# Recurrence outputs turned by VectorE in 32x32 blocks and put together by transfers, with the norm weight applied at the split

## The chip, the cores and the metric

The kernel runs on one core of one Trainium2 chip. The metric is the device time of one execution in microseconds (us), as the median of several runs. The engines are named as in the profile: PE is TensorE (matrix multiply; PEld is its weight load), DVE is VectorE, ACT is ScalarE, POOL is GpSimd, SP is SyncE, which computes nothing here and issues transfers. ACT and POOL issue transfers too; each issuing engine has a queue of its own and works through it in order.

## The reference, cut to what matters

One layer of a hybrid trunk on x of 2048 positions by 1024 channels, all in float32: a pooling branch and a gated recurrence branch, merged by gates, an output projection, a convolutional gated feed-forward layer, and a last norm. The change is in the recurrence branch, between the recurrence's outputs and the projection `w_pb`:

```python
def hgrn2_mixer(zq, zf, zi, zo, lb, norm_g):
    # q, f, k, v of 4 heads of 128 channels; S_t = diag(f_t) S_{t-1} + k_t v_t^T; o_t = S_t^T q_t
    ...
    o = o * lax.rsqrt(jnp.mean(o * o, axis=-1, keepdims=True) + EPS) * norm_g.astype(jnp.float32)
    o = o * jax.nn.silu(heads(zo))
    return o.reshape(B, S, HGRN_WIDTH).astype(zq.dtype)

yb = hgrn2_mixer(zq, zf, zi, zo, lower_bounds[l], hgrn_norm_g[l]) @ w_pb[l]
```

`norm_g` has one weight per channel of a head, the same for all four heads.

## The kernel before, in words

The 2048 positions are worked through in blocks of `TB` = 512. A pass of the outer loop takes two blocks (`b0` and `b0 + 1`, called `hf` 0 and 1): `mixer(b0)` does both branches up to the residual, `ffn(b0)` the feed-forward layer. There are two passes, so two mixers. Products of float32 numbers are split into a high part in the type `fp32r` and a low rest, and done as three matmuls (high-high, high-low, low-high); pairs of blocks are multiplied in a seven-product scheme (`P1` to `P7`), whose sums go through a few PSUM banks (X, Z, V) that VectorE and ScalarE read between the products.

Matmuls of this kind are issued by `mm`, which counts them: after every `MM_PER_TICK` = 6 it runs one `tick`, which converts one more weight tile (`stream.advance`) and steps the waiting tasks. A task is a Python generator; `yield n` lets n ticks pass before it goes on. Weights come through `raw` tiles, loaded on SP's queue (L198) and split by ScalarE (L245) and VectorE (L246) into `ops`. The instructions of each engine are then put in order by a scheduler that follows the program's order and its own estimate of when operands are ready; `first`, `second`, `behind` and `in_turn` are hints of the program to it. The 77 slots of on-chip memory and the eight PSUM banks are handed out the same way.

`hgrn_task(b, h, ...)` does the recurrence for one block and one head; three `runner` tasks work through the eight of a mixer, in between the matmuls of the gate projections (`gr`), so there are 16 in all. The last lines of each task:

- `po` (PSUM) holds the outputs of four chunks of 128 positions side by side: partition = position in the chunk, column = chunk * 128 + channel.
- four DVE instructions (L1169) multiply by the reciprocal root and by the output gate `zt` and write `ot`;
- after four ticks TensorE transposes the four 128x128 squares into the bank `pt` (L1175), so that partition = channel, column = position;
- ScalarE reads `pt` and multiplies by the norm weight, which is a number per partition now (`oh`, L1177), and issues the store to the DRAM tile `od` (`spill`, L987).

`o_task` starts with the second half of the pooling branch's projection (`pa`). It loads the eight `od` on SP's queue into `oT` (`fetch`, L992), waits until `place` reaches `O_PLACE`, and splits them into `oTs` high and low (L680 ScalarE, L681 VectorE), one every two ticks. `branch("pb", ...)` multiplies them by `w_pb`, first two chains of 12 matmuls on the block `hf` 0, then two on `hf` 1, then the rest. While `pa` runs, VectorE's `pa_u` (L1230) reads the bank `pa_Z` between two products that write it.

Of the kernel before, what the change touches and what calls it, by code (L numbers as in the profile page):

```python
# [11 lines left out]
F32 = mybir.dt.float32  # L12
F32R = mybir.dt.float32r
U8 = mybir.dt.uint8
AF = mybir.ActivationFunctionType
ALU = mybir.AluOpType
AX = mybir.AxisListType

P = 128
# [10 lines left out]
TB = 512  # L30
NT = TB // P
# [51 lines left out]
def tile_trunk(  # L83
# [16 lines left out]
    pe, act, dve, pool, sp = nc.tensor, nc.scalar, nc.vector, nc.gpsimd, nc.sync  # L100
# [6 lines left out]
    dram = ctx.enter_context(tc.tile_pool(name="dram", bufs=1, space=bass.MemoryType.DRAM))  # L107
    banks = ctx.enter_context(tc.tile_pool(name="banks", bufs=8, space=bass.MemoryType.PSUM))

    def slot(name, cols=TB, dt=F32):  # L110
        return slots.tile([P, cols], dt, tag="s", name=name, padded_shape=[P, 528])

    def bank(name, cols=512):
        return banks.tile([P, cols], F32, tag="b", name=name, padded_shape=[P, 512])

    def f32(ap):
        return ap.bitcast(F32)
# [467 lines left out]
    ident = const.tile([P, P], F32, tag="ident", name="ident")  # L585
# [9 lines left out]
    o_n1, o_n2, o_bg, o_ps, o_lb, o_hg, o_cb, o_cw = offs  # L595
# [8 lines left out]
    def col(o):  # L604
        return cols[:, o : o + 1]
# [68 lines left out]
    def split(src, name, on_pool=False):  # L674
        hi = slot(name + "h", TB, F32R)
        lo = slot(name + "l", TB, F32R)
        if on_pool:
            up = pool.tensor_scalar(hi, src, 1.0, 0.0, ALU.mult, ALU.add)
        else:
            up = act.copy(hi, src)  # L680
        low = dve.tensor_tensor(lo, src, f32(hi), ALU.subtract)  # L681
        last_split[0] = up, low
        return hi, lo
# [301 lines left out]
    def spill(t, name):  # L985
        d = dram.tile([P, TB], F32, tag=name, name=name)
        act.dma_start(d, t)  # L987
        return d

    def fetch(d, name, eng=sp):  # L990
        t = slot(name)
        eng.dma_start(t, d)  # L992
        return t


    def hgrn_task(b, h, d, q, vd, zd, od):
        def head_of(src, key):
            t = slot(f"{key}{b}_{h}")
            sp.dma_start(t.rearrange("p (c v) -> p c v", c=NT), src[:, :, h * P : (h + 1) * P])
            return t  # L1000
# [166 lines left out]
        ot = slot(f"ot{b}_{h}")  # L1167
        for c in range(NT):
            dve.scalar_tensor_tensor(ot[:, c * P : (c + 1) * P], po[:, c * P : (c + 1) * P],  # L1169
                                     r[:, c : c + 1], zt[:, c * P : (c + 1) * P],  # L1170
                                     ALU.mult, ALU.mult)
        yield 4
        pt = bank(f"pt{b}_{h}")
        for c in range(NT):
            pe.transpose(pt[:, c * P : (c + 1) * P], ot[:, c * P : (c + 1) * P], ident)  # L1175
        t = slot(f"oh{b}_{h}")
        act.activation(t, pt, AF.Copy, scale=col(o_hg))  # L1177
        od[b, h] = spill(t, f"od{b}_{h}")


    go_up, go_io = [False], [False]
# [114 lines left out]
    def add_forms(two, forms, k, name, store=lambda p, t: None, sums=True, pin=lambda i: None,  # L1296
                  eng=pool):

        def comb(p, x0, x1, op):
            if (p, k) in forms or x0 is None or x1 is None:  # L1300
                return
            t = slot(f"{name}_{p}_{k}")
            pin(eng.tensor_tensor(t, x0, x1, op))  # L1303
            forms[p, k] = t
            store(p, t)

        for p, at in (("P1", (1, 0)), ("P2", (1, 1)), ("P4", (0, 1))):
            if (p, k) not in forms and at in two:
                forms[p, k] = two[at]
                store(p, two[at])  # L1310
        if not sums:
            return
        comb("P7", two.get((1, 0)), two.get((0, 0)), ALU.subtract)
        comb("P5", two.get((0, 0)), two.get((0, 1)), ALU.subtract)
        comb("P6", forms.get(("P5", k)), two.get((1, 0)), ALU.subtract)
        comb("P3", forms.get(("P6", k)), two.get((1, 1)), ALU.add)
# [84 lines left out]
    def mixer(b0, forms, late):  # L1401
# [4 lines left out]
        md, od, gd = {}, {}, {}  # L1406
# [11 lines left out]
        def runner():  # L1418
            while taken[0] < 2 * HEADS:
                if queue:  # L1420
                    taken[0] += 1
                    yield from hgrn_task(*queue.pop(0))
                else:
                    yield 1
# [124 lines left out]
        oT = {}  # L1549
# [70 lines left out]
        def evac_b(m, hf, g, ps):  # L1620
            gated(g, hf, g, ps)
            dve.tensor_tensor(y[m, hf], y[m, hf], g, ALU.add)
            if m >= KD // 2 and hf:
                k = m - KD // 2
                two = {(h, r): y[k + r * (KD // 2), h] for h in range(2) for r in range(2)}
                add_forms(two, yf, k, f"yf{b0}", eng=dve)

        def o_task():
            t = {}
            for hf in range(2):  # L1630
                for g in range(HEADS):
                    while (b0 + hf, g) not in od:
                        yield 1
                    t[hf, g] = fetch(od[b0 + hf, g], f"oT{b0 + hf}_{g}")
            while place[0] < O_PLACE:
                yield 1
            for hf in range(2):
                for g in range(HEADS):
                    oT[hf, g] = split(t[hf, g], f"oTs{b0 + hf}_{g}")
                    yield 2  # L1640

        otask = []
        for d in range(2):
            units = [Unit(f"pa{b0}_{2 * d + e}", "pa", emit_a(2 * d + e)) for e in range(2)]
            for p in ORDER:
                place[0] += 1
                if (d, p) == (1, "P1"):
                    otask.append(Task(o_task()))
                for s_, hf in {"P6": ((1, 1),), "P5": ((0, 0),), "P7": ((1, 0),),
                               "P2": ((0, 1),)}.get(p, ()):  # L1650
                    for e in range(2):
                        gate(0, 2 * d + e + KD // 2 * s_, hf)
                while len(pf[FORM[p]]) < 2:
                    place[0] += 1
                    mtask.step()
                w = stream.get("pa")
                for e in range(2):
                    units[e].products(p, pf, pf[FORM[p]], w[:, :, e * 256 : e * 256 + 256])
                    units[e].after(p)
                stream.used(1)  # L1660
# [282 lines left out]
    for b in range(0, SEQ // TB, 2):  # L1943
        forms, task, late = nxt
        if b:
            join(task)
        forms, task, late = mixer(b, forms, late)
        join(task)
        nxt = ffn(b, forms, late)
# [50 lines left out]
```

## Time and profile before

| | |
|---|---|
| median of 3 runs | 2505.35 us (2504.9 to 2505.46) |
| profiled execution, first to last instruction | 2503.3 us |
| median less that span | 2.05 us |
| mean granted TensorE clock in it | 0.999 |
| the first `pt` transposes of the first mixer, the last ones | 199.3 us, 456.8 us |
| the last `pt` transposes of the second mixer | 1694.9 us |
| `pb` of the first mixer starts | 481.3 us |

The profiled execution's own time is known by its span alone. In a row of a group stand line, engine, operation, tiles (out<-in), count, then durations in ns as least / median / most, or busy us and mean ns of one. A row of the timeline begins with its start and its length in us. A row of a wait gives total us, times and the longest. Tile names leave out the numbers of block and head.

### The profile page before, as it was taken

The numbers are of one execution on the slowest core, as the hardware profiler recorded it, in microseconds if no ns is written. First come the engines' busy times: TensorE is split into PE (matmuls) and PEld (weight loads), VectorE is DVE, ScalarE is ACT, GpSimd is POOL, SyncE is SP. The second block draws the span as 40 slices with busy tenths as digits, with TensorE's granted clock in tenths as the row PEclk, the third lists the DMA queues.
The fourth block names the chain that finished last, engine by engine and source line by source line (L and its number), as shares of the span: only waits on it lengthen the run. The fifth ranks groups of instructions, "written<-read, shape, count | busy, mean of one in ns | idle before, by whom it ended". The sixth has DMA issues, their size and how long they took to land.

```text
span 2503.3 us, 35640 instructions
## 1 busy us (share of the span) xinstructions
PE 2490.4 (99%) x11428; PEld 2039.1 (81%) x11428; DVE 1977.8 (79%) x3510; ACT 1201.1 (48%) x2264; POOL 805.1 (32%) x1139
## 2 busy tenths in 40 slices
PE   9999999999999999999999999999999999999998
PEld 7888888888888888888888888887888888888887
DVE  7778768997998778885596777679979887778755
ACT  6534443435555545553554344443365555445534
POOL 4343353403354333451320202223033433325410
PEclk9999999999999999999999999999999999999999
DMA  8888788688888789897344343447443454447852
GB/s 276 271 206 247 227 229 242 210 243 251 202 255 238 226 228 243 263 366 244 122 152 152 118 127 110 143 141 259 135 148 122 153 150 138 149 137 247 319 165 100
DMA packets 257691, 497.68 MB, mean 199 GB/s; under 512 B 26912, under 2 KB 47520, under 8 KB 257184
## 3 DMA queue, kind: packets, MB, share of 16 engines
q1 hardware_dynamic: 189872, 317.53, 40.0%
q0 software_dynamic: 42656, 112.74, 17.7%
q10 hardware_dynamic: 24976, 65.13, 7.5%
q8 instruction: 90, 1.47, 0.2%
q14 instruction: 97, 0.79, 0.1%
HBM read 383.63 MB, written 189.27 MB: 229 GB/s over the span
## 4 chain that ended last, share of the span: by engine, by line
PE 97%; DVE 1%; ACT 0%; DMA 0%; issue 0%; POOL 0%; SPq 0%; ACTq 0%; DVEq 0%
PE dn_P L149 17%; PE up_Z L149 15%; PE up_X L149 10%; PE up_V L149 10%; PE wo_P L149 6%; PE gr_Z L149 5%; PE gr_X L149 4%; PE gr_V L149 4%; PE pb L149 4%; PE io_Z L149 3%; PE fr_Z L149 3%; PE fr_X L149 2%; PE fr_V L149 2%; PE io_V L149 2%; PE pl L1057 2%; PE ur_Z L149 1%
## 5 line engine op out<-in xcount | busy, mean ns | idle before, releaser
L245 ACT CAST ops<-raw 128x512 fp32r<-128x512 f32 x792 | 489.3, 621 | 826.4 <-PE dn_P L149 176.6
L246 DVE TENSOR_TENSOR ops<-raw,ops 128x512 fp32r<-128x512 f32 x792 | 590.4, 749 | 202.8 <-ACT ops L245 198.4
L1734 DVE SCALAR_TENSOR_TENSOR e<-h,cols,e 128x512 f32<-128x512 f32 x176 | 143.4, 819 | 30.9 <-ACT e L1732 23.7
L1732 ACT ACTIVATE e<-h,cols 128x512 f32<-128x512 f32 x176 | 142.2, 814 | 25.1 <-DVE h L1190 18.2
L1737 DVE SCALAR_TENSOR_TENSOR e<-h,cols,e 128x512 f32<-128x512 f32 x176 | 134.0, 771 | 2.5
L992 POOL DMA_DIRECT2D g_P<-dg_P x154 | 83.8, 545 | 160.7 <-PE dn_P L149 112.1
L1303 POOL TENSOR_TENSOR gf_P<-e,e 128x512 f32<-128x512 f32 x44 | 61.1, 1391 | 149.4 <-DVE e L1743 95.9
L467 POOL TENSOR_TENSOR raw<-raw,raw 128x512 f32<-128x512 f32 x36 | 49.1, 1363 | 157.6 <-DVE ops L246 124.5
L1303 POOL TENSOR_TENSOR gf_P<-gf_P,e 128x512 f32<-128x512 f32 x44 | 59.2, 1345 | 71.8 <-DVE e L1743 71.4
L1727 POOL COPY h<-h 128x2 f32<-128x2 f32 x88 | 40.5, 472 | 117.3 <-DVE h L1189 110.4
L1443 POOL TENSOR_TENSOR q<-q,qs 128x512 f32<-128x512 f32 x16 | 22.1, 1380 | 166.3 <-ACT qs L1442 163.9
L1741 ACT ACTIVATE e<-e 128x512 f32<-128x512 f32 x88 | 55.6, 632 | 39.6 <-DVE e L1737 39.3
L1729 POOL COPY hist<-h 128x2 f32<-128x2 f32 x88 | 35.3, 402 | 118.9 <-DVE h L1190 117.1
L1190 DVE TENSOR_TENSOR h<-up_u,up_V 128x512 f32<-128x512 f32 x88 | 60.1, 683 | 10.2 <-PE up_V L149 9.7
L1278 DVE TENSOR_TENSOR x<-x,wo_P 128x512 f32<-128x512 f32 x88 | 56.0, 684 | 6.7 <-PE wo_P L149 6.3
L1476 ACT ACTIVATE gt<-gt,cols 128x512 f32<-128x512 f32 x48 | 34.9, 726 | 53.1 <-DVE gt L1190 39.5
L1278 DVE TENSOR_TENSOR ac<-ac,dn_P 128x512 f32<-128x512 f32 x72 | 47.1, 683 | 16.7 <-PE dn_P L149 16.3
L1042 POOL COPY qm<-q 128x64 f32<-128x64 f32 x64 | 27.1, 446 | 98.4 <-DVE q L1048 19.9
L1228 ACT COPY up_e<-up_X 128x512 f32<-128x512 f32 x44 | 25.8, 587 | 59.5 <-PE up_X L149 52.3
L1727 POOL COPY h<-hist 128x2 f32<-128x2 f32 x88 | 45.1, 519 | 28.5 <-DVE m_T42l L681 28.5
L1757 POOL DMA_DIRECT2D dg_P<-gf_P x88 | 50.7, 576 | 8.1 <-POOL gf_P L1303 7.4
L1057 PE MATMUL pl<-qm,k 128*128 128x192 f32 x256 | 50.0, 325 | 0.0
(1335 smaller groups left out, 8061.8 us busy)
## 6 DMA issues: line engine op xcount, KB each, us to landing
g_P<-dg_P POOLq DMA_DIRECT2D x154, 256.0 KB, 6.2
raw<-in_w_up_t SPq DMA_DIRECT2D x132, 256.0 KB, 3.3
raw<-in_w_in_t SPq DMA_DIRECT2D x98, 256.0 KB, 3.6
dg_P<-gf_P POOLq DMA_DIRECT2D x88, 256.0 KB, 4.0
dg_P<-e SPq DMA_DIRECT2D x66, 256.0 KB, 3.5
raw<-in_w_dn SPq DMA_DIRECT2D x66, 256.0 KB, 3.8
x<-in_x SPq DMA_DIRECT2D x64, 256.0 KB, 5.2
gd<-gt ACTq DMA_DIRECT2D x64, 256.0 KB, 2.7
```

The source lines that it names most:

```text
L149: count[1] = pe.matmul(*args, **kw)
L245: self.mark = act.copy(hi, v)
L246: low = self.low = dve.tensor_tensor(lo, v, f32(hi), ALU.subtract)
L992: eng.dma_start(t, d)
L1057: ins = pe.matmul(pa_[:, c * 192 : c * 192 + 192], ks[:, (i + c) * P : (i + c + 1) * P], mv[:, c].rearrange("p s x -> p (s x)"), start=Tru ...
L1190: return dve.tensor_tensor(dst, t, ps, ALU.add if how == "add" else ALU.subtract)
L1278: dve.tensor_tensor(t, t, ps[j], ALU.add if sg > 0 else ALU.subtract)
L1303: pin(eng.tensor_tensor(t, x0, x1, op))
L1727: pool.tensor_copy(h[:, 0:2], hist[:, mt] if hf == 0 else hs[s, 0][:, TB : TB + 2])
L1732: in_turn(act.activation(t, h[:, 2:], AF.Identity, bias=col(o_cb + mt), scale=col(o_cw + 4 * MF + mt)))
L1734: in_turn(second(dve.scalar_tensor_tensor(t, h[:, 1 : 1 + TB], col(o_cw + 2 * MF + mt), t, ALU.mult, ALU.add)))
L1737: dve.scalar_tensor_tensor(t, h[:, 0:TB], col(o_cw + mt), t, ALU.mult, ALU.add)
```

## The change

VectorE turns `ot` with one instruction per task (`blocks_turned`): it transposes each of the 4 x 16 blocks of 32x32 within itself. A block stays on its 32 partitions, so the result `oz` has each block turned, but the blocks not yet in their places. Four transfers on SP's queue (`blocks_moved`), one for each band of 32 partitions, write them to `od` with the bands put where a whole transpose has them: each is 32 partitions by four runs of 128 elements (512 bytes), 64 KB. The transpose is issued right after `ot`, the transfers two ticks later; before, the transposes came four ticks after `ot`.

In `od` a row is a channel as before, but its columns stand in the order position-in-chunk * 4 + chunk. `split_turned` undoes that order: it reads `oT` with a stride of four elements and writes contiguous halves. It also applies the norm weight, which the task no longer does: the high half is a scaled copy on ScalarE, the low half one VectorE instruction that scales and subtracts.

```diff
+    def blocks_turned(t, name):
+
+        z = slot(name)
+        dve.transpose(z.rearrange("p (b j c) -> p b c j", b=4, c=NT),
+                      t.rearrange("p (c b i) -> p b c i", c=NT, b=4))
+        return z
+
+    def blocks_moved(dst, z, eng=sp):
+
+        d = dst.rearrange("(b i) (a m) -> a i b m", b=4, a=4)
+        for a in range(4):
+            eng.dma_start(d[a], z[32 * a : 32 * a + 32].rearrange("i (b m) -> i b m", b=4))
...
-        yield 4
-        pt = bank(f"pt{b}_{h}")
-        for c in range(NT):
-            pe.transpose(pt[:, c * P : (c + 1) * P], ot[:, c * P : (c + 1) * P], ident)
-        t = slot(f"oh{b}_{h}")
-        act.activation(t, pt, AF.Copy, scale=col(o_hg))
-        od[b, h] = spill(t, f"od{b}_{h}")
+        oz = blocks_turned(ot, f"oz{b}_{h}")
+        yield 2
+        d = dram.tile([P, TB], F32, tag=f"od{b}_{h}", name=f"od{b}_{h}")
+        blocks_moved(d, oz)
+        od[b, h] = d
...
+        def split_turned(t, name):
+            hi, lo = (slot(name + c, TB, F32R) for c in "hl")
+            v = t.rearrange("p (m c) -> p c m", c=NT)
+            h4, l4 = (x.rearrange("p (c m) -> p c m", c=NT) for x in (hi, lo))
+            act.activation(h4, v, AF.Copy, scale=col(o_hg))
+            dve.scalar_tensor_tensor(l4, v, col(o_hg), f32(h4), ALU.mult, ALU.subtract)
+            return hi, lo
+
...
-                    oT[hf, g] = split(t[hf, g], f"oTs{b0 + hf}_{g}")
+                    oT[hf, g] = split_turned(t[hf, g], f"oTs{b0 + hf}_{g}")
```

## The prediction

> **What bounds the kernel now.** I read the page first, for the busy shares and the chain that ended last; then TensorE's waits; then the rows of the tile `pt`, which the change takes away.
>
> ```profile
> span 2503.3 us, 35640 instructions
> PE 2490.4 (99%) x11428; PEld 2039.1 (81%) x11428; DVE 1977.8 (79%) x3510; ACT 1201.1 (48%) x2264; POOL 805.1 (32%) x1139
> PE 97%; DVE 1%; ACT 0%; DMA 0%; issue 0%; POOL 0%; SPq 0%; ACTq 0%; DVEq 0%
> ...
> PE x_t L744 <- DVE x_xs L738: 2.9, 4, 1.1
> PE warm L706 <- POOL ident L587: 1.4, 1, 1.4
> PE pa_Z L149 <- DVE pa_u L1230: 0.9, 2, 0.5
> PE io_Z L149 <- ACT ops L245: 0.6, 1, 0.6
> ```
>
> TensorE (PE) is busy 99% of the span and is 97% of the chain of waits. The last four lines are all of its waits: 5.8 us in total. So work taken off TensorE shortens the kernel by about what it occupied, as long as nothing starts to make TensorE wait; and the reverse holds too, since no idle time is left there to hide a new wait.
>
> What the transposes occupy is not their duration, because matmuls overlap. I read it from the starts in the timeline of TensorE around one group of four (start, duration, in us):
>
> ```profile
> L1175 PE MATMUL pt<-ident,ot x64: 270/272/274, 199.3 to 1694.9; 128*128 128x128 f32 x64
> L1177 ACT ACTIVATE oh<-pt,cols x16: 678/687/689, 200.0 to 1697.1; 128x512 f32<-128x512 f32 x16
> ...
> 198.87 0.39 PE L149 MATMUL gr_Z<-x_T22h,ops 128*128 128x512 f32 x1
> 199.10 0.40 PE L149 MATMUL gr_Z<-x_T23h,ops 128*128 128x512 f32 x1
> 199.33 0.60 PE L1175 MATMUL pt<-ident,ot 128*128 128x128 f32 x4
> 199.69 0.48 PE L149 MATMUL gr_Z<-x_T23l,ops 128*128 128x512 f32 x1
> 200.00 0.40 PE L149 MATMUL gr_Z<-x_T23h,ops 128*128 128x512 f32 x1
> ```
>
> Without transposes a 512-column matmul starts 0.23 us after the one before (198.87, 199.10, 199.33). With the group, `x_T23l` starts at 199.69 instead of 199.33, and its successor 0.31 us later instead of 0.23: together 200.00 - 199.33 - 0.23 = 0.44 us. There are 64 / 4 = 16 groups: 16 x 0.44 = **7.0 us** of TensorE.
>
> **The change, part by part.** *Removed from TensorE:* the 7.0 us above, and nothing is added there. This is the main term: -7.0 us.
>
> *ScalarE (ACT):* 16 evictions `oh` of 0.687 us (11.0 us) and 16 store issues go. The eight splits per mixer get a scaled, strided first half instead of a plain copy. The nearest row to that first half is `oh` itself, a scaled copy of the same size: 0.69, about what the plain copy costs, so ACT's sum falls by some 11 us. ACT is at 48% and releases none of TensorE's waits but one of 0.6 us near the start; I cost it at nothing. Its cover is its own idle time; without that, 16 first halves a little late would each hold up a chain of `pb`.
>
> *VectorE (DVE):* 16 block transposes are added, and the 16 `oTs` low halves read with a stride of four elements and take a scale. No row shows a block transpose. The bounds, from other DVE rows:
>
> ```profile
> L738 DVE TENSOR_SCALAR m_xs<-x,m_2r x8: 474/480/486, 591.4 to 1854.1; 128x512 f32<-128x512 f32 x8
> L681 DVE TENSOR_TENSOR oTs_1l<-oT,oTs_1h x4: 679/1229/1776, 478.0 to 1730.3; 128x512 fp32r<-128x512 f32 x4
> L1734 DVE SCALAR_TENSOR_TENSOR e<-h,cols,e 128x512 f32<-128x512 f32 x176 | 143.4, 819 | 30.9 <-ACT e L1732 23.7
> L1127 DVE TENSOR_TENSOR f<-f 128x128 f32<-128x128 f32 x16 | 9.0, 561 | 0.1
> L1048 DVE TENSOR_TENSOR q<-qm,f 128x128 f32<-128x128 f32 x64 | 17.1, 287 | 0.4 <-ACT qm L1041 0.4
> ...
> sum 590.00, PE 589.54 PEld 491.34 DVE 461.54 ACT 261.60 POOL 193.78; mean PE 42.11 PEld 35.10 DVE 32.97 ACT 18.69 POOL 13.84
> ```
>
> Lower bound of a transpose: 0.48 us, the fastest 128x512 instruction (one source). Upper: 1.78 us, the longest of a tile that is split here. I take 0.7 us, nearest to the undisturbed 128x512 minimum of 0.68, because the same 512 elements per partition pass. The low half goes from 0.68 to some 0.82 (the row of L1734, same operation and size). Upper bound: L1127 in this form strides by four elements and takes 561 ns where the mostly contiguous L1048 takes 287, so 0.69 x 561 / 287 = 1.35 us. Added work: 16 x (0.7 + 0.14) = 13 us, at most 16 x (1.78 + 0.67) = 39 us. The last line sums fourteen stretches of the two mixers (180 to 460 and 1430 to 1740 us): DVE is idle there 590.0 - 461.5 = 128 us. On the mean it fits three times over. Locally it need not:
>
> ```profile
> 454.21 0.68 DVE L1230 TENSOR_TENSOR pa_u<-pa_e,pa_Z 128x512 f32<-128x512 f32 x1
> 454.81 1.12 DVE L1169 SCALAR_TENSOR_TENSOR ot<-po,ro,z 128x128 f32<-128x128 f32 x4
> 455.84 0.68 DVE L1230 TENSOR_TENSOR pa_u<-pa_e,pa_Z 128x512 f32<-128x512 f32 x1
> 456.49 0.60 PE L1175 MATMUL pt<-ident,ot 128*128 128x128 f32 x4
> 456.85 0.48 PE L149 MATMUL pa_Z<-mf0T30h,ops 128*128 128x512 f32 x1
> ```
>
> This is the last head of the first mixer. The transpose belongs right behind the four `ot`, so ahead of the second `pa_u`, and the matmul `pa_Z` at 456.85 may write its bank only when that `pa_u` has read it. Now `pa_u` ends at 456.52, and the four `pt` transposes fill TensorE until then. After the change TensorE is there at 456.49, while `pa_u` ends 0.7 us later, at 457.2: a wait of 0.7 us, at most 1.8. The other mixer has the same place. For the other 14 transposes I find no such neighbour; I allow nothing for them, and give them the whole of the second rival. Lower end, from freed banks (`pt` held one of eight) and from `pa_u` coming out luckier: -0.9, the whole of today's `pa_Z` waits. I take 2 x 0.5 = +1.0 us, between nothing (if `pa_u` is ordered first) and the 0.7.
>
> *SP's queue:* 16 stores leave ACT's queue and come back as 64 on SP's, each of 64 KB in 512-byte runs. The nearest rows are `wb` (512-byte runs, stored) and `v` (512-byte runs, loaded):
>
> ```profile
> L983 SPq DMA_DIRECT2D wb<-cw x16: 513/572/647, 168.5 to 353.0; - x16
> v<-vd SPq DMA_DIRECT2D x16, 256.0 KB, 4.3
> od<-oh ACTq DMA_DIRECT2D x16, 256.0 KB, 3.7
> SPq L198 <- DVE ops L246: 1384.4, 621, 11.1
> q1 hardware_dynamic: 189872, 317.53, 40.0%
> ...
> 457.06 2.81 SPq L992 DMA_DIRECT2D oT<-od  x2
> 469.12 0.33 SPq L198 DMA_DIRECT2D raw<-in_w_pb_t  x1
> ...
> 471.27 2.61 SPq L992 DMA_DIRECT2D oT<-od  x5
> ...
> 481.30 0.39 PE L149 MATMUL pb<-oTs_0h,ops 128*128 128x512 f32 x1
> ```
>
> Issue: 64 x 0.57 = 37 us at most (0.3 each at least, as the 0.33 of a plain `raw` row, 21 us). SP spends 1384 us waiting for `ops` to free a raw buffer, so 37 us beside it are free. The added wait: a store stands on SP until its transpose is done, and behind it stand the weight loads `raw`. The store comes two ticks of six matmuls after the transpose, 12 x 0.23 = 2.8 us, which is longer than the 1.78 of the upper bound, so SP should find it done. POOL's queue is not touched.
>
> *The path that sets the end of a mixer:* the last `ot` ends at 455.93. Transpose to 456.6 (upper 457.7), store issued no earlier than two ticks later, 458.7, four issues of 0.57 to 461.0, landing 4.3 later: 465.3. The last `oT` load is issued at about 473.5 (the row of five ends at 473.88). The cover is 8 us; if it were gone, `pb`, from 481.30 on, would wait for the rest.
>
> *DMA engines:* 16 x 512 = 8192 runs replace 16 x 128 = 2048. At q1's mean (0.400 x 16 x 2503.3 us / 189,872 = 84 ns) the surplus is 6144 x 0.084 / 16 = 32 us of all engines, an upper bound because those packets are 1.7 KB in the mean; over the 590 us of the mixers 5%. Loads run ahead by several buffers, so I cost it at nothing.
>
> Sum against the profiled execution: 2503.3 - 7.0 + 1.0 = 2497.3. The runs' median, 2505.35, lies 2.05 us above that span; the same distance gives **2499.3 us**, 0.24% less. About 0.2% (5.0 us) is what a measurement of this kernel can tell from no change.
>
> **The rivals.**
>
> *Eaten up (no measurable change).* Transposes in front of evictions at more places than the two I found. For: the DVE rows from 454.21 to 456.52 stand without a gap. Against: of its 3510 instructions TensorE waits for six. With 0.2 us at the other 14, 2.8 us: 2499.3 + 2.8 = 2502.1.
>
> *Slower: the transpose is long and DVE is in order.* One mechanism, at the `ot` of every head: TensorE waits for evictions queued behind the transpose. Break-even is a mean wait of 7.0 / 16 = 0.44 us per transpose; slower by 0.2% from (7.0 + 5.0) / 16 = 0.75 us. At the bound of 1.78 us with 0.7 us absorbed, 1.1 us each: 2505.35 - 7.0 + 17.6 = 2516. Against it: the waits' 5.8 us, and the 128 us idle. The Trainium skill (VectorE: DVE Perf Modes, Rules for kernel authors) sides with it in general: TensorE is its choice for a 128x128 transpose where PSUM will do as the destination. The trace speaks against that here, since TensorE is at 99% and DVE at 79%.
>
> *Slower: the strided move is very slow.* If these transfers took 19 times the 3.7 us of `od<-oh`, 70 us, the last would land at 461 + 70 = 531, and the load that follows some 4.3 later, at 535. `pb` starts at 481.30 with two chains of 12 matmuls on the first block, so it needs the second from 481.3 + 24 x 0.23 = 487 on: a wait of 48 us in each mixer, 2499.3 + 96 = 2595. Against it: `v` with its runs of 512 bytes lands in 4.3 us. That factor is from the Trainium skill (VectorE: DVE Perf Modes, The three transpose paths), for a plain copy whose access pattern does the transpose; the trace's `v` disagrees for runs of 512 bytes.
>
> *Better than the sum:* no new wait, and today's 0.9 us on `pa_u` gone too: 2505.35 - 7.0 - 0.9 = 2497.4.
>
> **How the numbers follow.** Forecast 0.58, eaten up 0.26, slower by the long transpose 0.08, by the slow move 0.01, better 0.07. Faster by over 0.2%: 0.58 + 0.07 = 0.65; within 0.2%: 0.26; slower: 0.09. The range takes in the better case and most of the second: 2496.5 (0.9 below the better case, for shifts in the order) to 2504.0; the slower cases and some 0.08 of the rest lie outside.
>
> **What would show it.** Right: `pt` and `oh` gone, TensorE busy about 2483 us, its waits up by 1 us on `pa_u`; a transpose row of 0.5 to 1.8 us; `oTs` low halves at 0.8; the four `od` stores 0.3 to 0.6 us each on SP, landing within 8 us; the last `oT` load still near 466 to 474. Wrong: new waits of TensorE on `pa_u`, `gr_u` or `ops` of more than 2 us, a transpose above 1.8 us, SP waiting for `oz` ahead of `raw`, or `pb` waiting for `oTs`.

## The result, and the profile after

The changed kernel takes 2510.43 us (median of 15 runs, 2508.44 to 2513.76) against 2505.15 for the kernel before (15 runs beside it). The ratio is 1.0021, 95% interval [1.0013, 1.0029]: 5.3 us slower. Forecast was 6.1 us faster. The runs of the change also lie further apart than those of the kernel before. From here on, medians are compared; the text gives the interval of each ratio, and 0.0009 of it is 2.3 us.

The profiled execution of the change is 3.5 us longer than that of the kernel before. From the page:

```profile
span 2506.8 us, 35575 instructions
PE 2485.6 (99%) x11364; PEld 2031.6 (81%) x11364; DVE 1998.6 (80%) x3526; ACT 1199.7 (48%) x2248; POOL 813.0 (32%) x1139
```

TensorE is busy 4.8 us less (2490.4 before), DVE 20.8 us more. What TensorE waits for, in total, times and longest:

```profile
PE pa_Z L149 <- DVE pa_u L1241: 3.8, 6, 1.0
PE x_t L744 <- DVE x_xs L738: 3.7, 4, 1.6
PE fr_Z L149 <- DVE fr_u L1241: 2.1, 1, 2.1
PE pb L149 <- DVE oTs_1l L1644: 1.6, 2, 0.8
PE warm L706 <- POOL ident L587: 1.4, 1, 1.4
PE io_Z L149 <- ACT ops L245: 0.6, 1, 0.6
PE gr_Z L149 <- DVE gr_u L1241: 0.5, 1, 0.5
```

5.8 us have become 13.7. Less busy by 4.8 and waiting 7.9 more, TensorE accounts for 3.1 of the 3.5 us. The wait on `x_xs` lies in the first 14 us, ahead of anything changed; over the profiles of all the runs below it comes to between 1.9 and 4.9 us. The new ones are on `pa_u` (+2.9), `fr_u` (+2.1), the low halves `oTs` (+1.6) and `gr_u` (+0.5). All are VectorE's. The rows of the new and the changed instructions (least, median, most in ns):

```profile
L999 DVE STREAM_TRANSPOSE oz<-ot x16: 1076/1098/1127, 195.5 to 1694.5; 128x512 f32<-128x512 f32 x16
L1643 ACT ACTIVATE oTs_2h<-oT,cols x4: 1202/1212/1215, 480.6 to 1729.9; 128x512 fp32r<-128x512 f32 x4
L1644 DVE SCALAR_TENSOR_TENSOR oTs_2l<-oT,cols,oTs_2h x4: 1108/1113/1124, 484.6 to 1735.7; 128x512 fp32r<-128x512 f32 x4
```

The transpose takes 1.10 us instead of the 0.7 I took, the low half 1.11 instead of 0.82, and the high half 1.21 instead of 0.69. Each takes one element in four on one side of it: the transpose writes with that stride, the halves read with it.

The timeline of the change at the place that the prediction pointed out, the last head of the first mixer:

```profile
454.73 0.68 DVE L1241 TENSOR_TENSOR pa_u<-pa_e,pa_Z 128x512 f32<-128x512 f32 x1
455.33 1.12 DVE L1182 SCALAR_TENSOR_TENSOR ot<-po,ro,z 128x128 f32<-128x128 f32 x4
456.49 1.09 DVE L999 STREAM_TRANSPOSE oz<-ot 128x512 f32<-128x512 f32 x1
457.43 0.67 DVE L1241 TENSOR_TENSOR pa_u<-pa_e,pa_Z 128x512 f32<-128x512 f32 x1
...
456.80 0.40 PE L149 MATMUL pa_Z<-mf0T31h,ops 128*128 128x512 f32 x1
458.15 0.50 PE L149 MATMUL pa_Z<-mf0T30h,ops 128*128 128x512 f32 x1 [0.96 <-DVE pa_u L1241]
```

The transpose stands between `ot` and the second `pa_u`, and `pa_Z` starts 1.35 us after the matmul before it instead of 0.23. That is the predicted wait, 0.96 us in each mixer; another 0.5 us stands ahead of it, for the `pa_u` at 454.73. Two others were not predicted. One is in `pb`, where the halves of the second block come too late from the sixth tile on:

```profile
495.63 2.07 DVE L1644 SCALAR_TENSOR_TENSOR oTs_1l<-oT,cols,oTs_1h 128x512 fp32r<-128x512 f32 x1
497.76 0.51 PE L149 MATMUL pb<-oTs_1l,ops 128*128 128x512 f32 x1 [0.81 <-DVE oTs_1l L1644]
```

This low half took 2.07 us and not 1.11; GpSimd adds two tiles (`ya`) from 493.87 to 496.86. Before the change the same half took 1.78 us instead of 0.68, also beside such additions, and `pb` did not wait. The other wait is at 360 us, and two engines have a part in it:

```profile
356.60 0.59 ACT L1239 COPY fr_e<-fr_X 128x512 f32<-128x512 f32 x1 [4.52 <-DMA od<-oz]
...
357.74 0.69 DVE L246 TENSOR_TENSOR ops<-raw,ops 128x512 fp32r<-128x512 f32 x1 [2.84 <-ACT ops L245]
358.35 1.08 DVE L999 STREAM_TRANSPOSE oz<-ot 128x512 f32<-128x512 f32 x1
359.27 0.67 DVE L956 TENSOR_TENSOR s<-s 128x512 f32<-128x512 f32 x1
359.86 0.67 DVE L1241 TENSOR_TENSOR fr_u<-fr_e,fr_Z 128x512 f32<-128x512 f32 x1
```

ScalarE stood until a store of `oz` had landed (its `fr_e` goes into a slot that `oz` held, as I read it). So VectorE stood idle for 2.8 us until its next operand was there, and then the transpose came ahead of `fr_u`.

### The profile page after: what moved, and what is told of

It is laid out like the page before. It is cut to its first block, busy times and chain, and to the rows that moved or that the text cites. A ratio compares the mean times of both kernels' runs of the same rounds, so it can differ in the third digit from the quotient of the medians.

```text
span 2506.8 us, 35575 instructions
## 1 busy us (share of the span) xinstructions
PE 2485.6 (99%) x11364; PEld 2031.6 (81%) x11364; DVE 1998.6 (80%) x3526; ACT 1199.7 (48%) x2248; POOL 813.0 (32%) x1139
## 4 chain that ended last, share of the span: by engine, by line
PE 91%; DVE 4%; DMA 2%; issue 2%; ACT 1%; POOL 0%; SPq 0%; ACTq 0%; DVEq 0%; POOLq 0%
PE dn_P L149 17%; PE up_Z L149 15%; PE up_X L149 10%; PE up_V L149 10%; PE wo_P L149 6%; PE gr_Z L149 5%; PE gr_X L149 3%; PE gr_V L149 3%; PE pb L149 3%; PE io_Z L149 3%; PE fr_Z L149 2%; PE io_V L149 2%; PE pl L1070 2%; PE fr_X L149 1%; PE fr_V L149 1%
## 5 line engine op out<-in xcount | busy, mean ns | idle before, releaser
L1055 POOL COPY qm<-q 128x64 f32<-128x64 f32 x64 | 34.1, 556 | 91.5 <-DVE q L1061 25.3
```

## The experiments

Three theories. **1:** the gain is the predicted 7.0 us, and VectorE's time gives it back and more: transposes in front of evictions, and halves made slow by the stride. **2:** the 64 stores cost, by SP's queue or by slots held until they land. **3:** the transposes of TensorE were worth less than 7.0 us.

**e2_no_turn: the gain alone.**

```diff
-            pe.transpose(pt[...], ot[...], ident)       # 4 of them, and the bank pt
-        act.activation(t, pt, AF.Copy, scale=col(o_hg))
+        act.activation(t, ot, AF.Copy, scale=col(o_hg))
```

> The kernel before, with TensorE's 64 transposes left out and nothing in their place: ScalarE scales ot and it is stored as it stands, so the recurrence outputs are not turned. It measures the gain by itself. Theory 1: -7.0 us, 2498.1 (16 groups x 0.44 us), TensorE's waits as before. Rival, that the removed time was partly cover for waits on VectorE: -4 to -5 us, with the difference as new waits on pa_u.

Measured 2500.86, ratio 0.9982 [0.9973, 0.9991]: -4.1 us, the rival's size. The profile of this run:

```profile
PE 2483.3 (99%) x11364; PEld 2031.8 (81%) x11364; DVE 1978.3 (79%) x3510; ACT 1200.8 (48%) x2264; POOL 805.7 (32%) x1139
...
PE pa_Z L149 <- DVE pa_u L1227: 2.2, 3, 1.3
```

TensorE is busy 7.1 us less than before (2490.4), which is the predicted 7.0. Its waits are 2.5 us longer: 1.3 in one new wait on `pa_u`, taken up at e5, and 1.2 on `x_xs`, which the edit does not touch.

**e3_dve_added: the transposes on VectorE alone.**

```diff
+        oz = slot(...)
+        dve.transpose(oz.rearrange("p (b j c) -> p b c j", ...), ot.rearrange("p (c b i) -> p b c i", ...))
         yield 4
         pt = bank(f"pt{b}_{h}")                         # as before from here
```

> The kernel before, whole, with the 16 block transposes of the change added on VectorE right behind ot; their result is not used. Nothing changes on SP or for the split. Theory 1: the transposes alone make TensorE wait, about 2 x 1.1 us at pa_u and 2 us at fr_u or the like: +3 to +5 us, 2508 to 2510. Theory 2: VectorE has room (128 us idle in the mixers), +0 to +1 us.

Measured 2511.37, 1.0024 [1.0015, 1.0034]: +6.4 us, more than expected. VectorE's and TensorE's rows at the second head, of the kernel before and of this one:

```profile
200.92 1.11 DVE L1169 SCALAR_TENSOR_TENSOR ot<-po,ro,z 128x128 f32<-128x128 f32 x4
201.96 0.67 DVE L1230 TENSOR_TENSOR gr_u<-gr_e,gr_Z 128x512 f32<-128x512 f32 x1
```

```profile
204.29 1.08 DVE L1173 STREAM_TRANSPOSE oz<-ot 128x512 f32<-128x512 f32 x1
205.22 0.67 DVE L1233 TENSOR_TENSOR gr_u<-gr_e,gr_Z 128x512 f32<-128x512 f32 x1
...
205.94 0.50 PE L149 MATMUL gr_Z<-x_T30h,ops 128*128 128x512 f32 x1 [2.07 <-DVE gr_u L1233]
```

Before, `gr_u` followed `ot` at once. Here the order of VectorE's list is another: the transpose and five instructions of the next head stand ahead of `gr_u`, and one wait of 2.1 us is the result. So an added instruction costs more than its length where it changes the order of its neighbours. In all, this profile has 3.8 us more of waits on `gr_u` and `pa_u`, and TensorE is busy 1.6 us longer, of a span that is 5.2 us longer.

**e4_split_only and e8_scale_only: the split alone, with and without the stride.** e4 is the kernel before with `split_turned` in the place of `split`. e8 has the scale without the stride:

```diff
+        act.activation(hi, t, AF.Copy, scale=col(o_hg))
+        dve.scalar_tensor_tensor(lo, t, col(o_hg), f32(hi), ALU.mult, ALU.subtract)
...
-        act.activation(t, pt, AF.Copy, scale=col(o_hg))
+        act.copy(t, pt)
```

> The kernel before, with the changed split alone: strided by four elements and scaled, on both engines (so the positions come out in another order and the weight is applied twice). Theory 1: the high half takes 1.2 us and the low half 1.1 us, TensorE waits for oTs some 1.6 us in each mixer: +3 us, 2508. Theory 2: the split is not it, +0 to +0.5 us.

> The kernel before with the norm weight moved to the split and nothing else: the transposes stay on TensorE, od keeps its order, the halves are read contiguously but with the scale. Theory 1 (the stride doubles the halves, the scale does not): high half 0.7, low half 0.7 to 0.8 us, 2505 +- 0.7. Rival (the scale, a scalar_tensor_tensor instead of a tensor_tensor, makes the low half slow): low half 1.1 us, 2508.

e4: 2508.38, 1.0013 [1.0004, 1.0023], +3.5 us. e8: 2505.44 against 2505.31, 1.0001 [0.9992, 1.0010]. A high and a low half in e8:

```profile
L1630 ACT ACTIVATE oTs_2h<-oT,cols x4: 707/715/722, 479.1 to 1729.6; 128x512 fp32r<-128x512 f32 x4
L1631 DVE SCALAR_TENSOR_TENSOR oTs_3l<-oT,cols,oTs_3h x4: 739/740/741, 484.8 to 1734.3; 128x512 fp32r<-128x512 f32 x4
```

TensorE's wait in e4, and the start of the same matmul of `pb` before and in e4:

```profile
PE pb L149 <- DVE oTs_1l L1633: 1.6, 2, 0.8
```

```profile
500.72 0.39 PE L149 MATMUL pb<-oTs_0h,ops 128*128 128x512 f32 x1
```

```profile
502.47 0.39 PE L149 MATMUL pb<-oTs_0h,ops 128*128 128x512 f32 x1
```

`pb` began 0.2 us later in e4 (481.5 instead of 481.3), so some 1.5 us were lost within it; twice that, for two mixers, is 3.0 of the 3.5 us (an estimate).

The scale costs little (0.71 us against 0.62 of the plain copy, 0.74 against 0.68); the stride is what makes 1.21 and 1.11 of it. The Trainium skill (SBUF — State Buffer, SBUF: two separate sides) speaks of lines of 16 bytes and of a penalty for each access that crosses to a new one. Four float32 are 16 bytes, so here every access does, and the trace agrees: 1.11 against 0.74. The same passage goes on to call a stride of up to 4 float32 free; if that is meant to take in this one, the measurement decides against it. A stride of two was free in the kernel before: L1127 on 256 elements, two apart, took 0.42 to 0.43 us in 15 of 16, which lies on the line between 0.29 for 128 contiguous elements and 0.68 for 512.

**e12_moves: the stores alone.**

```diff
-        od[b, h] = spill(t, f"od{b}_{h}")
+        blocks_moved(d, t)                              # 64 transfers on SP's queue
```

> The kernel before, whole, with the store alone changed: the transposed and scaled tile goes out by the change's 64 transfers on SP's queue instead of 16 on ScalarE's (so the bands come out in other places; the traffic is the change's). Theory 1: 2505 +- 1, since the sum of e2, e3 and e4 (-4.1, +6.4, +3.5) already gives the change's +5.3 within 0.5 us. Theory 2 (the stores cost by their queue and their landing): 2507 or more.

Measured 2504.39, 0.9996 [0.9988, 1.0005]. The 64 stores cost nothing that can be measured, and theory 2 falls as far as queue and traffic go. It has no wait on `fr_u`, so it does not test the landing for which ScalarE stood 4.5 us in the change; that remains, with an unknown part of the 2.1 us on `fr_u`. SP did stand waiting for `oz` in the change:

```profile
od<-oz SPq DMA_DIRECT2D x64, 64.0 KB, 2.1
...
SPq L1007 <- DVE oz L999: 29.8, 13, 4.8
```

No weight came late for it: of TensorE's waits after, only the old 0.6 us is on `ops`.

**e6_act_queue: the change with its stores on ScalarE's queue.**

```diff
-        blocks_moved(d, oz)
+        blocks_moved(d, oz, act)
```

> The changed kernel with its 64 stores issued on ScalarE's queue instead of SP's; all else as in the change. Theory 1 (the stores' queue is not the cost): 2510 +- 1. Theory 2 (weight loads behind the stores on SP's queue are late): 2505 to 2508. A third possibility: 64 issues on ScalarE's queue delay its copies, 2512 or more.

Measured 2516.10, 1.0041 [1.0028, 1.0054], the third possibility.

```profile
PE pa_Z L149 <- DVE pa_u L1241: 6.0, 5, 2.4
PE fr_Z L149 <- DVE fr_u L1241: 3.0, 1, 3.0
```

```profile
359.13 0.62 ACT L245 CAST ops<-raw 128x512 fp32r<-128x512 f32 x1 [5.39 <-DMA od<-oz]
359.78 0.69 DVE L246 TENSOR_TENSOR ops<-raw,ops 128x512 fp32r<-128x512 f32 x1 [4.91 <-ACT ops L245]
```

ScalarE stood 13.1 us in all for landings of the stores (5.4 in the change), and VectorE waited for its copies. Whether the issues themselves held the copies up as well is not shown apart. The queue of the engine that computes nothing was the cheaper place.

**e1_runs: the change without the stride.** The transpose writes rows of 32 elements; ScalarE puts them in order, scaled, by one copy; the split is the plain one.

```diff
-        dve.transpose(z.rearrange("p (b j c) -> p b c j", b=4, c=NT),
+        dve.transpose(z.rearrange("p (b c j) -> p b c j", b=4, c=NT),
...
+            act.activation(u.rearrange("p (c a j) -> p c a j", a=4, c=NT),
+                           t.rearrange("p (a c j) -> p c a j", a=4, c=NT), AF.Copy, scale=col(o_hg))
+            return split(u, name)
```

> The changed kernel, but nothing reads or writes single elements with a stride any more: the block transpose writes its 32-element rows next to each other (order band, chunk, position in od), and before the split one ScalarE instruction per tile copies the tile into position order in runs of 32 elements and scales it; the split is then the plain one of the kernel before. 16 ScalarE instructions more, no change for TensorE. Theory 1 (VectorE's time is the cost: the strided halves took 1.12 us instead of 0.68, and the transposes stand in front of evictions): the low halves are back at 0.68, TensorE's wait on oTs goes (-3 us), the transpose takes 0.7 to 1.1 us; some 2507 against the change's 2510.4, with the waits on pa_u still there. Theory 2 (the 64 stores on SP's queue and their landing are the cost): they are unchanged, so 2510 +- 1.

Measured 2503.93, 0.9995 [0.9986, 1.0004]: 6.5 us less than the change, and the wait on `oTs` is gone. Theory 1 had expected 2507; the run has the shorter transposes besides the contiguous halves, and does not part the two. Its profile is of one of its longer executions (2505.88).

```profile
L999 DVE STREAM_TRANSPOSE oz<-ot x16: 691/710/714, 196.5 to 1693.7; 128x512 f32<-128x512 f32 x16
L1641 ACT ACTIVATE oTs_2u<-oT,cols x4: 715/719/722, 484.6 to 1730.0; 128x512 f32<-128x512 f32 x4
...
PE pa_Z L149 <- DVE pa_u L1241: 3.5, 5, 1.3
PE fr_Z L149 <- DVE fr_u L1241: 1.6, 1, 1.6
```

The transpose is 0.71 us now. The waits on `pa_u` and `fr_u` remain.

**e5_later and e7_later_act: the transposes later.** To e1, two ticks between `ot` and the transpose; in e7 the stores on ScalarE's queue besides.

```diff
+        yield 2
         oz = blocks_turned(ot, f"oz{b}_{h}")
```

> e1_runs with the block transpose issued two ticks (2.8 us) after ot instead of right behind it, and the stores two ticks after that. Same work on every engine. Theory 1 (it is the place in VectorE's order, ahead of evictions, that makes TensorE wait): the waits on pa_u and fr_u fall from 5.1 us to below 3, some 2501.5 against 2503.9. Rival (any 0.7 us added to VectorE in these stages costs, wherever it stands): 2503 to 2505.

> e5_later with the 64 stores on ScalarE's queue. If both places matter, it is the fastest of the turned versions, 2500 to 2501; if the queue does not, it equals e5_later within 1 us; if ScalarE's queue is the tighter one, it is 1 to 3 us slower than e5_later.

e5: 2502.54, 0.9989 [0.9980, 0.9998]. e7: 2507.18, 1.0008 [0.9999, 1.0017], 4.6 us above e5 where at most 3 had been expected; again ScalarE's queue is the worse one. e5 is below the kernel before and below the change, but its distance from e1 is within the intervals. By its time e5 lies between theory 1 (2501.5) and the rival (2503 to 2505). The wait on `fr_u` is gone and the transposes stand behind `pa_u`, yet 4.1 us on `pa_u` remain, where theory 1 had expected less than 3. (TensorE's granted clock was 0.947 in this one profile, so I use its order and its waits on VectorE, not its span.) GpSimd, VectorE and TensorE in e5:

```profile
453.52 2.96 POOL L467 TENSOR_TENSOR raw<-raw,raw 128x512 f32<-128x512 f32 x2 [4.68 <-DVE ops L246]
...
453.53 1.82 DVE L681 TENSOR_TENSOR mf0T40l<-mf_t,mf0T40h 128x512 fp32r<-128x512 f32 x1
455.27 0.67 DVE L1242 TENSOR_TENSOR pa_u<-pa_e,pa_Z 128x512 f32<-128x512 f32 x1
...
456.09 0.48 PE L149 MATMUL pa_Z<-mf0T30h,ops 128*128 128x512 f32 x1 [1.87 <-DVE pa_u L1242]
```

and the same two instructions before the change:

```profile
453.77 3.04 POOL L467 TENSOR_TENSOR raw<-raw,raw 128x512 f32<-128x512 f32 x2 [4.49 <-DVE ops L246]
...
453.61 0.68 DVE L681 TENSOR_TENSOR mf0T40l<-mf_t,mf0T40h 128x512 fp32r<-128x512 f32 x1
```

VectorE's low half of `mf T40` and GpSimd's first addition of two collide. Before the change VectorE started 0.16 us ahead and took 0.68 us. In e5 the two start within 10 ns of each other, and VectorE's instruction, which stands right ahead of `pa_u`, takes 1.82 us. e2_no_turn has both outcomes from the same starts, in its second and in its first mixer:

```profile
1687.09 2.97 POOL L467 TENSOR_TENSOR raw<-raw,raw 128x512 f32<-128x512 f32 x2 [4.10 <-DVE ops L246]
...
1687.10 1.83 DVE L681 TENSOR_TENSOR mf2T40l<-mf_t,mf2T40h 128x512 fp32r<-128x512 f32 x1
```

```profile
450.77 3.21 POOL L467 TENSOR_TENSOR raw<-raw,raw 128x512 f32<-128x512 f32 x2 [4.08 <-DVE ops L246]
...
450.78 0.69 DVE L681 TENSOR_TENSOR mf0T40l<-mf_t,mf0T40h 128x512 fp32r<-128x512 f32 x1
```

So the start that the trace shows does not tell which of them goes first. But one always pays: where VectorE took 1.83 us the first addition alone took 1.29, and where VectorE took 0.69 it took 1.84.

The Trainium skill (SBUF — State Buffer, SBUF: two separate sides) has a port pair that a VectorE instruction with two inputs there shares with GpSimd: whoever starts first holds it for the whole instruction, and the other is blocked. The trace agrees, with these two pairs.

**e9_t4_later, e10_before_t4, e11_no_turn_t4: that place moved**, in e5, in the kernel before and in e2.

```diff
-                yield from reach(8 + 2 * j)
+                yield from reach(10 + j)                # in pa_task, form T4
```

> e5_later with one place moved besides: the first sum of the pooling branch's form T4 and its split (mf T40) are issued two products later, behind both pa_u instead of ahead of the first. Theory 1 (what is left of the cost is the low half of mf T40: it and an addition on GpSimd are released by the same VectorE instruction, and when GpSimd starts first it takes 1.82 us instead of 0.69, just ahead of pa_u): the wait on pa_u, 4.1 us in e5_later, falls below 1.5 us, some 2500 against e5_later's 2502.5, and the runs lie closer together. Rival (some other instruction takes its place ahead of pa_u): 2502 to 2504.

> The control: the kernel before with that one place moved and no other change. There the low half of mf T40 started ahead of GpSimd's addition and took 0.68 us. Theory 1: 2505.0 +- 0.5. If it is below 2504, what e9_t4_later gains is not owed to the turning.

> e2_no_turn (TensorE's transposes left out and nothing in their place, so the outputs are not turned) with the place of mf T40 moved. Theory 1 (the 64 transposes are worth 7.0 us, and in e2_no_turn some 3 us came back as the slow mf T40): 7.0 us below e10_before_t4, some 2498. Rival (the transposes are worth 4 us): 2501.

e10: 2506.25, 1.0003 [0.9994, 1.0012]. e11: 2499.26, 0.9975 [0.9966, 0.9985]. Their difference is -7.0 us, with no wait on the two `pa_u` at this place in either. But e10 came out 1.2 us above the kernel before, outside the 2505.0 +- 0.5 expected of it, and e11 lies 5.8 us below the kernel before. All of these differences agree within their intervals, some 3 us, so the medians leave 4 to 7 us open; what carries the 7.0 is the sum from the starts and TensorE's busy time, 7.1 us less in e2. Nor was the slow `mf T40` the whole of the missing 3 us in e2: its wait is 1.3. e9: 2503.90, 0.9994 [0.9986, 1.0003], no gain over e5. The first `pa_u` is in time there, and the wait has moved to the one that follows, as the rival had it:

```profile
PE pa_Z L149 <- DVE pa_u L1246: 3.2, 4, 1.4
...
PE pa_Z L149 <- DVE pa_u L1242: 0.9, 2, 0.5
```

Of the versions that do the whole computation, e5_later is the fastest: 2.8 us below the kernel before, ratio 0.9989 [0.9980, 0.9998], and not told apart from e1 and e9.

## Why the prediction was wrong, point by point

The step that failed is the price of VectorE's added work: +1.0 us at two places and nothing elsewhere, where the runs show +6.4 for the transposes and +3.5 for the halves. Three of the signs that the prediction named for being wrong came: more than 2 us of new waits on `pa_u` (2.9), SP waiting for `oz`, and `pb` waiting for `oTs`.

*The gain of TensorE, 7.0 us: right as busy time, not as it arrives.* TensorE is busy 7.1 us less in e2; the medians give 4.1 (e2 in the code as it stands), 5.8 (e11) or 7.0 (e11 less e10). Theory 3 is not excluded by the medians alone. In the change itself TensorE was busy 4.8 us less, 2485.6 where about 2483 was forecast; part of that is that a wait also lengthens what follows it (at 497.76 us the next matmul starts 0.35 us later instead of 0.23).

*The transposes, "16 x 0.7", and "for the other 14 I allow nothing": wrong, and the larger miss.* The duration was 1.10, inside the bounds. The price was +6.4 us alone (e3), of which my two places were the 2 x 0.5. My search for neighbours read the order of the kernel before, and that order was not kept. That is 6.4 / 16 = 0.40 us of time per transpose (the new waits alone are 3.8 us), just under the 0.44 that I gave as break-even: by itself this would have used up nearly all of the gain.

*The split, "from 0.68 to some 0.82" and a high half that costs "about what the plain copy costs": the second miss, of +3.5 us (e4).* The row that showed the stride's price was in the prediction (561 ns against 287), and I set its 1.35 us aside as an end of the range and took the row without a stride. I also scaled it wrongly. The 561 ns are a mean that three of the 16 draw up (0.89, 1.49 and 1.49 us); the other 13 take 0.37 to 0.44 us. Their surplus over the contiguous 0.29 is some 0.1 us for 128 elements, 0.4 for 512: 0.68 + 0.4 = 1.1 us (an estimate), which is what was measured. For ScalarE I had taken no bound for the stride at all. And I counted these microseconds on the mean of the mixers, where they fit, instead of at `pb`, whose halves had come just in time.

*The rival "the transpose is long and DVE is in order" asked for 0.75 us per transpose.* It had the right engine and the right direction, but the wait per transpose did not reach that; the slow halves were needed with it.

*Stores and queue at nothing: right* (e12). Landing at nothing is not shown: ScalarE stood 4.5 us for one ahead of the wait on `fr_u`. "SP should find it done" was wrong, with 29.8 us of waiting; the cover by SP's other waiting held. The rival of the slow move is out: 64 KB land in 2.1 us (median). Its 70 us had no row behind them.

The parts add up: -4.1 + 6.4 + 3.5 - 0.7 = +5.1 against +5.3 measured. Each part is known within some 2.3 us, so that they meet to 0.2 is luck; that transposes and halves together exceed the gain is not. What stays open: in the change's own profile `mf T40` took 0.69 us in both mixers, and that execution is among its faster ones. There VectorE and GpSimd start together (both at 454.12 us), where VectorE had a lead of 0.16 us before. That the spread of the change's runs is this race would fit, but one profile cannot show it. Another part goes with the clock: its eight executions with a granted clock of 0.998 have a median of 2510.7 us, the seven with 0.999 one of 2509.1. And why ScalarE stood 4.5 us for a landing in the change and in e1, and not in e5, I have read from the order only.

## What to carry to other kernels

Work taken off the engine that bounds a kernel is worth what its starts in the timeline say; what it is replaced by has to be priced at the places where the bounding engine waits for the other one within a microsecond, not against that engine's idle sum. An added instruction also reorders its neighbours, so run the added part alone before the whole. When rows disagree on a price, take the row whose access pattern is that of the new instruction, look at its single durations and not at a mean, and where possible write the layout so that the last step reads contiguous runs.

## What the runs showed of the hardware that I had not expected

Reading or writing 512 float32 per partition with a stride of four elements takes VectorE 1.11 us instead of 0.74 and ScalarE 1.21 instead of 0.71; a block transpose of 128x512 takes 1.10 us with such a stride on its output and 0.71 with runs of 32. A stride of two elements cost nothing (256 elements in 0.42 us, where 128 contiguous ones took 0.29 and 512 took 0.68). A VectorE instruction with two inputs from on-chip memory and a GpSimd addition that started within 10 ns of it took either 1.82 and 1.28 us or 0.69 and 1.84.
